# SwiGLU's gate and up as seven block products instead of eight, with the down projection in four chunks between the next chunk's pairs

## The chip, the cores and the metric

The kernel runs on one core of one Trainium2 chip. The metric is the device time of one execution in microseconds (us). Five engines matter here: TensorE (PE, with its weight loads listed apart as PEld), VectorE (DVE), ScalarE (ACT), GpSimd (POOL) and SyncE (SP), whose queue issues the loads. Each engine runs its own queue in order and waits on semaphores for the others.

## The reference

A decoder trunk of two layers on x of 512 tokens by 1024 features, all in float32:

```python
for i in range(2):
    x = x + 0.5 * swiglu(rmsnorm(x, ffn1_norm[i]), ffn1_w_gate[i], ffn1_w_up[i], ffn1_w_down[i])
    h = rmsnorm(x, mix_norm[i])
    o, o_mem = ...            # layer 0: gated linear attention, layer 1: latent attention; memory attention
    x = x + jnp.concatenate([o, o_mem], axis=-1) @ w_out[i]
    x = x + 0.5 * swiglu(rmsnorm(x, ffn2_norm[i]), ffn2_w_gate[i], ffn2_w_up[i], ffn2_w_down[i])

def swiglu(h, w_gate, w_up, w_down):
    return (jax.nn.silu(h @ w_gate) * (h @ w_up)) @ w_down
```

There are four SwiGLU blocks. In each, gate and up are 1024 x 2816 and down is 2816 x 1024.

## The kernel before

x lies transposed in SBUF: eight tiles of 128 features by 512 tokens, `x0` to `x7`. Every product keeps float32 accuracy by splitting both factors into a rounded high part and the exact rest: `mm3` issues three matmuls, high x high, high x low and low x high, all summed into one PSUM bank.

The weights come as a stream of units, 128 x 1024 each (eight blocks of 128 x 128). `load_unit` loads a unit into a `raw` tile through SP, `split_weights` makes `wh` (a cast on ACT) and `wl` (a subtraction on DVE). There are four slots for `wh` and four for `wl`, so splitting can run three units ahead of the one that PE is using.

A SwiGLU block (`ffn`) has two chunks of 11 blocks of 128 hidden features. For each block f, `project` sums the gate over the eight input tiles into one bank and the up into another; each takes one unit: 24 matmuls of 512 columns. `gate_up` scales by 1/rms, applies Silu, multiplies and splits the result. After 11 blocks the down projection runs over that chunk: for each of eight output tiles d, 11 blocks of three matmuls each, then `xadd` adds to x. The last chunk's `xadd` goes on into the next norm: `Norm.split` makes the scaled high and low parts of a tile (one ACT and one DVE instruction of 512), `Norm.square` adds up the squares, and `Norm.finish` gets 1/rms by Newton steps on DVE, whose result the gates wait for and PE does not.

The order of the instructions is planned: each of these pieces is a flow, a generator that yields instructions, and the flows are merged by the time at which an instruction could start by the planner's costs. The builder's own scheduler has the last word, and each engine then runs the result in order.

Of the kernel before, what the change touches and what calls it, by code (L numbers as in the profile page):

```python
# [17 lines left out]
P = 128  # L18
# [8 lines left out]
NCH = 2  # L27
FCH = NFT // NCH
# [9 lines left out]
NRAW, NSPL, NTMP = 3, 4, 64  # L38
NHEAD = 4
NLATE = 5  # L40

# [38 lines left out]
class Opening:  # L80
    """The first product into a bank that several flows sum into; the others come after it."""
# [23 lines left out]

class Engine:
    """An engine whose methods give instructions to be emitted later."""
# [4 lines left out]
    def __getattr__(self, method):  # L112
        real = getattr(self.eng, method)

        def make(*args, **kw):
            aps = [a for a in args if _is_ap(a)]
            outs = [kw[k] for k in ("out", "accum_out") if _is_ap(kw.get(k))]
            if "out" not in kw:
                outs.append(aps.pop(0))
            ins = aps + [v for k, v in kw.items() if k not in ("out", "accum_out") and _is_ap(v)]  # L120
            cost, lat = self.price(method, kw, outs, ins)
            return Op(self.name, lambda: real(*args, **kw), cost, [a.name for a in ins], [a.name for a in outs], lat)  # L122

        return make

    def price(self, method, kw, outs, ins):
        n = max([_n_free(outs[0])] + ([_n_free(ins[0])] if method == "tensor_reduce" else []))
        if self.name == "PE":
            passes = 1 if ins[0].dtype == F32R else 4
            n = _n_free(kw["rhs"]) if "rhs" in kw else P  # L130
            return passes * n / 2.4 + 3, 200
        if self.name == "ACT":
            return 110 + 0.833 * n, 200
# [9 lines left out]
        if single and not any(_in_psum(a) for a in ins[:1] + outs[:1]):  # L143
            return 60 + 0.65 * n, 130
        return 60 + 1.06 * n, 130


class Flows:
    def __init__(self, tiles):
        self.tiles = tiles  # kind -> (function of the dtype, slots)  # L150
        self.free_at = {k: deque([0.0] * n) for k, (_, n) in tiles.items()}
        self.kind, self.clock, self.wr, self.rd = {}, {}, {}, {}
        self.flows, self.count = [], 0
# [4 lines left out]

    def done(self, *tiles):
        for t in tiles:  # L160
            k = self.kind.pop(t.name)
            self.free_at[k].append(max(self.wr.get(t.name, 0.0), self.rd.get(t.name, 0.0)))
# [11 lines left out]
    def advance(self, f, value=None):  # L174
        """Runs a flow to its next instruction, wait or need."""
# [7 lines left out]
    def settle(self):  # L183
        """Gives the tiles and flags that can be given now."""
        moved = True
        while moved:
            moved = False
            for f in sorted(self.flows, key=lambda f: f[:2]):
                while True:
# [6 lines left out]
                    elif isinstance(w, Take) and len(self.free_at[w.kind]) > w.spare:  # L196
                        q = self.free_at[w.kind]
                        at = min(q)
                        q.remove(at)
                        t = self.tiles[w.kind][0](w.dt)  # L200
                        self.kind[t.name] = w.kind
                        self.rd[t.name] = at
# [7 lines left out]
    def run(self):  # L210
        while True:
# [4 lines left out]
            for f in self.flows:  # L216
                if isinstance(f[3], Op):
                    k = (self.start(f[3]), f[0], f[1])
# [17 lines left out]
def _emit(tc, ctx, xT, memT, wflat, sizes, cst, out):  # L236
    nc = tc.nc
    const = ctx.enter_context(tc.tile_pool(name="const", bufs=1))
    wraw = ctx.enter_context(tc.tile_pool(name="wraw", bufs=NRAW))
    wsp = ctx.enter_context(tc.tile_pool(name="wsp", bufs=NSPL))  # L240
# [6 lines left out]
        "t": (lambda dt: tp.tile([P, 512], dt, tag="t", name="t"), NTMP),  # L247
# [39 lines left out]
    units = [[Flag(), None, Flag(), None] for _ in sizes]  # L287
# [3 lines left out]
    def load_unit():  # L291
        u, n = units[ahead[0]], sizes[ahead[0]]
# [5 lines left out]
        u[1], u[0].set = raw, True  # L298

    def split_weights():  # L300
        for u, n in zip(units, sizes):
            yield u[0]
            h = yield Take("wh", F32R, 0)
            l = yield Take("wl", F32R, 0)
            yield A.copy(out=h[:, :n], in_=u[1][:, :n])
            yield V.tensor_tensor(out=l[:, :n], in0=u[1][:, :n], in1=h[:, :n].bitcast(F32), op=ALU.subtract)
            done(u[1])
            u[3], u[2].set = (h, l), True

    at = [0]  # L310
# [3 lines left out]
    class Blocks:  # L314
        """The next n blocks of the stream, w columns each, per blocks in a unit."""
# [4 lines left out]
        def next(self):  # L320
            j = self.i % self.per
            if j == 0:
                self.end()
                u = units[at[0]]
                assert sizes[at[0]] == min(self.per, self.n - self.i) * self.w, at
                at[0] += 1
                yield u[2]
                self.cur = u[3]
# [26 lines left out]
    def newton_rsqrt(dst, src, scale, hv, y, t):  # L355
        """dst = (src * scale + EPS) ** -0.5, of a guess from the exponent and Newton steps."""
# [13 lines left out]
    def wide_rsqrt(acc, n):  # L370
        """(the sum of acc over its partitions / n + EPS) ** -0.5, on all partitions."""
# [8 lines left out]
    def bcast(ps, col):  # L380
        """col [P tokens, NJ] -> ps [P, S], the value of each token on all partitions."""
# [10 lines left out]
    def colsum(ps, acc, n):  # L392
        """Sums over partitions of acc [P, n*P], onto the partitions of ps' columns."""
# [4 lines left out]
    class Norm:  # L398
        """x times the gain in two parts, and 1/rms of each token."""

        def __init__(self, gname, layer):
            self.g = (gname, layer * KD)
            self.layer, self.by_token = layer, gname == "mx"
            self.h, self.l = [None] * KD, [None] * KD
            self.part = [Flag() for _ in range(KD)]
            self.summed = [Flag() for _ in range(KD)]
# [3 lines left out]
        def add(self, k):  # L410
            yield from self.split(k)
            yield from self.square(k)

        def split(self, k):
            yield xin[k]
            lo = self.g[1] + k
            g = C(self.g[0], lo, lo + 1)
            h = yield tt(F32R)
# [3 lines left out]
            self.h[k], self.l[k], self.part[k].set = h, l, True  # L422

# [31 lines left out]
        def free(self):  # L455
            done(*self.h, *self.l)

    def project(ps, nrm):
        """ps [P features, S] = a column block of weights on the normed x (without 1/rms)."""
        blk = Blocks(KD, P, KD if at[0] else KD // NHEAD)  # L460
# [8 lines left out]
    def xadd(d, ps, scale, nxt, last):  # L469
        """x += scale * ps; what follows from it."""  # L470
# [13 lines left out]
    def ffn(nrm, nxt, last):  # L484
        def gate_up(f, pg, pu):
            yield nrm.ready
            g = yield tt()
            yield V.tensor_tensor(out=g, in0=pg, in1=nrm.bc, op=ALU.mult)
            done(pg)
            yield A.activation(out=g, in_=g, func=AF.Silu)  # L490
            u = yield tt()
            yield V.tensor_tensor(out=u, in0=pu, in1=nrm.bc, op=ALU.mult)
            done(pu)
            yield V.tensor_tensor(out=u, in0=u, in1=g, op=ALU.mult)
            done(g)
            h = yield tt(F32R)
            l = yield tt(F32R)
            yield from split(u, h, l)
            done(u)
            hid[f][1:] = [h, l]  # L500
            hid[f][0].set = True

        for c in range(NCH):
            hid = [[Flag(), None, None] for _ in range(FCH)]
            for f in range(FCH):
                pg = yield bank(1)
                yield from project(pg, nrm)
                pu = yield bank(1)
                yield from project(pu, nrm)
                spawn(gate_up(f, pg, pu))  # L510
            end = c == NCH - 1
            if end:
                nrm.free()
            blk = Blocks(KD * FCH, P, KD)
            for d in range(KD):
                ps = yield bank(1)
                for f in range(FCH):
                    wh, wl = yield from blk.next()
                    yield hid[f][0]
                    yield from mm3(ps, wh, wl, hid[f][1], hid[f][2], f == 0, f == FCH - 1)  # L520
                spawn(xadd(d, ps, 0.5, nxt if end else None, last and end))
            blk.end()
            for _, h, l in hid:
                done(h, l)
# [17 lines left out]
    def token_project(nrm, width, per, spare=2):  # L542
        """Projection with tokens on the partitions; as many tiles of tokens in a bank as fit."""
# [26 lines left out]
    def head_scale(ps, out, rs, rs2, m):  # L570
        """ps is raw [P tokens, 4 x 128], m tiles of tokens; out is ps with each 128 at an rms of 1."""
# [19 lines left out]
    def mem_prep(l, mp):  # L591
        """The memory times its gain in two parts, and 1/rms of its tokens."""
# [33 lines left out]
    class Mem:  # L626
# [93 lines left out]
        def half(self, h, b, po, ends, opening):  # L720
            """One head and two tiles of queries."""
# [91 lines left out]
    def gla(l, nrm, nxt):  # L813
# [15 lines left out]
        def decays(ps):  # L829
            """The gates' logarithms, summed within each chunk."""  # L830
# [32 lines left out]
        def head(h, pk, pq, pv):  # L863
# [40 lines left out]
            # scores of two chunks at a time, keys on the partitions  # L904
# [532 lines left out]
```

## Time and profile before

| what | value |
|---|---|
| time, median of 3 runs | 2079.43 us (2078.87 to 2079.77) |
| profiled execution, first to last instruction (span) | 2077.5 us |
| instructions | 24715 |
| PE / PEld busy | 2060.4 us (99%) / 1700.3 us (82%) |
| DVE busy | 1106.5 us (53%) |
| ACT busy | 723.1 us (35%) |
| POOL busy | 45.1 us (2%) |
| DMA | 192.76 MB, mean 93 GB/s |
| granted TensorE clock | 1.000 |

The profiled execution's own time is not listed beside the runs; its span is 1.9 us under their median, and the rest is what lies around the first and last instruction. Busy is the share of the span in which an engine works. Matmuls overlap, so the mean time of one (390 ns) is longer than the distance from one to the next, and a busy PE says only that there was always one in flight.

### The profile page before, as it was taken

The page shows a single profiled execution, that of the slowest core. Times are in us where ns is not written, and L with a number is a line of the kernel's source. Part 1 is how long each engine was busy: PE and PEld are TensorE (multiplying, and loading weights), DVE is VectorE, ACT ScalarE, POOL GpSimd, SP SyncE. Part 2 cuts the span into 40 slices and gives each one's busy share as a digit, 9 for nine tenths or more (in the row PEclk, how much of TensorE's full clock was granted, in tenths as well). Part 3 has the DMA queues.
Part 4 walks back from the last instruction along what each step waited for, and adds up shares of the span by engine and source line. Part 5 has one row for each costly group of instructions (what it writes and reads, how often), then busy time and mean ns, then how long its engine had stood idle before and what let it go on. Part 6 is the DMA issues. An engine that isn't in the chain of part 4 may idle for free.

```text
span 2077.5 us, 24715 instructions
## 1 busy us (share of the span) xinstructions
PE 2060.4 (99%) x9806; PEld 1700.3 (82%) x9806; DVE 1106.5 (53%) x1952; ACT 723.1 (35%) x1167; POOL 45.1 (2%) x121
## 2 busy tenths in 40 slices
PE   8999999999999999999999999999999999999999
PEld 6888888878988888888888888889876878888887
DVE  7443444548875744344464434445887657433442
ACT  5222233444442432223332223334576433222321
POOL 0000000000000000000000000000031100000000
PEclk9999999999999999999999999999999999999999
DMA  5323232313212223232333232323211213323231
GB/s 187 102 92 102 91 101 95 117 63 102 82 60 73 93 100 100 93 102 92 102 103 101 93 102 92 101 91 118 84 44 41 72 61 102 101 92 102 91 107 66
DMA packets 55988, 192.76 MB, mean 93 GB/s; under 512 B 6208, under 2 KB 8384, under 8 KB 55872
## 3 DMA queue, kind: packets, MB, share of 16 engines
q1 hardware_dynamic: 55584, 189.92, 27.9%
q8 instruction: 77, 1.26, 0.2%
q10 hardware_dynamic: 288, 1.26, 0.2%
q14 instruction: 39, 0.32, 0.0%
HBM read 189.05 MB, written 2.10 MB: 92 GB/s over the span
## 4 chain that ended last, share of the span: by engine, by line
PE 96%; DVE 2%; ACT 0%; issue 0%; DMA 0%; SPq 0%; POOL 0%; DVEq 0%; ACTq 0%
PE ps L122 96%; DVE s L122 1%; DVE wl L122 1%; DVE t L122 1%; ACT t L122 0%; DMA x<-xT 0%; SPq L122 0%; POOL t L122 0%; ACT wh L122 0%; DVE x L122 0%; DVE ps L122 0%; DVEq L122 0%; ACTq L122 0%
## 5 line engine op out<-in xcount | busy, mean ns | idle before, releaser
L122 PE MATMUL ps<-t,wh 128*128 128x512 f32 x4864 | 1507.4, 391 | 6.0 <-ACT wh L122 5.5
L122 PEld LDWEIGHTS ps<-t,wh 128*128 128x128 f32 x4864 | 912.5, 188 | 203.4 <-issue 6.7
L122 PE MATMUL ps<-t,wl 128*128 128x512 f32 x2432 | 949.1, 390 | 0.5 <-DVE wl L122 0.5
L122 ACT CAST wh<-raw 128x1024 fp32r<-128x1024 f32 (+3 forms) x361 | 370.0, 1027 | 1029.7 <-PE ps L122 650.3
L122 DVE TENSOR_TENSOR wl<-raw,wh 128x1024 fp32r<-128x1024 f32 (+3 forms) x361 | 430.0, 1192 | 243.0 <-ACT wh L122 242.5
L122 PEld LDWEIGHTS ps<-t,wl 128*128 128x128 f32 x2432 | 457.0, 188 | 97.3 <-issue 2.7
L122 DVE TENSOR_TENSOR t<-ps,t 128x512 f32<-128x512 f32 (+3 forms) x241 | 156.7, 656 | 471.9 <-PE ps L122 453.7
L122 PE MATMUL ps<-wh,t 128*128 128x256 f32 (+3 forms) x928 | 215.5, 320 | 0.0
L122 DVE TENSOR_TENSOR t<-t 128x512 f32<-128x512 f32 (+1 forms) x290 | 197.5, 688 | 11.9 <-ACT t L122 1.4
L122 PEld LDWEIGHTS ps<-wh,t 128*128 128x128 f32 x928 | 155.8, 190 | 10.2 <-issue 2.1
L122 PE MATMUL ps<-wl,t 128*128 128x256 f32 (+3 forms) x464 | 148.8, 321 | 0.0
L122 PE MATMUL ps<-t 128*128 128x128 f32 (+6 forms) x760 | 141.4, 329 | 0.9 <-ACT t L122 0.6
L122 DVE SCALAR_TENSOR_TENSOR x<-ps,x 128x512 f32<-128x512 f32 x96 | 66.0, 689 | 135.9 <-PE ps L122 135.9
L122 PEld LDWEIGHTS ps<-t 128*128 128x128 f32 (+1 forms) x760 | 98.0, 190 | 32.7 <-issue 16.9
L122 PEld LDWEIGHTS ps<-wl,t 128*128 128x128 f32 x464 | 88.3, 190 | 5.2 <-issue 1.1
L122 ACT ACTIVATE t<-t 128x512 f32<-128x512 f32 x124 | 76.2, 625 | 24.9 <-DVE t L122 24.8
L122 ACT CAST t<-t 128x512 fp32r<-128x512 f32 x96 | 59.9, 625 | 62.4 <-DVE t L122 62.4
L122 PE MATMUL ps<-cs,t 128*128 128x128 f32 x312 | 52.0, 276 | 5.7 <-DVE t L122 3.2
L122 PEld LDWEIGHTS ps<-cs,t 128*128 128x128 f32 x312 | 36.7, 141 | 21.6 <-issue 7.5
L122 ACT ACTIVATE t<-x,cs 128x512 fp32r<-128x512 f32 x48 | 34.3, 721 | 53.3 <-DVE x L122 49.4
L122 ACT COPY t<-ps 128x256 f32<-128x256 f32 (+3 forms) x86 | 36.3, 436 | 30.0 <-PE ps L122 26.7
L122 ACT ACTIVATE t<-ps 128x512 f32<-128x512 f32 (+3 forms) x64 | 30.3, 485 | 42.6 <-PE ps L122 42.5
(69 smaller groups left out, 558.7 us busy)
## 6 DMA issues: line engine op xcount, KB each, us to landing
raw<-wflat SPq DMA_DIRECT2D x341, 512.0 KB, 3.4
raw<-wflat SPq DMA_DIRECT2D x12, 192.0 KB, 2.4
x<-xT SPq DMA_DIRECT2D x8, 256.0 KB, 5.0
t<-memT SPq DMA_DIRECT2D x8, 256.0 KB, 4.1
out<-x SPq DMA_DIRECT2D x8, 256.0 KB, 2.0
raw<-wflat SPq DMA_DIRECT2D x4, 448.0 KB, 3.2
cm<-cst ACTq DMA_DIRECT2D x1, 640.0 KB, 4.1
cm<-cst ACTq DMA_DIRECT2D x1, 585.5 KB, 4.4
```

Source lines behind the costliest of these rows:

```text
L122: return Op(self.name, lambda: real(*args, **kw), cost, [a.name for a in ins], [a.name for a in outs], lat)
```

## The change

**Gate and up.** Two hidden blocks f, f+1 are taken together (a pair), and the product is done for both by 2 x 2 blocks: the weights are cut into an upper and a lower half of the input features and into gate and up; the normed x into an upper and a lower half of the features (tiles 0 to 3 and 4 to 7) and into the first and the last 256 tokens. Seven products of sums of such blocks replace the eight. One product has four input tiles by two hidden blocks, three matmuls each: 24 matmuls of 256 columns.

**Weights.** The four units of a pair arrive as they are. On DVE four additions of 128 x 1024 make the sums, and each of the seven factors is then split by a cast on ACT and a subtraction on DVE.

**The other factor.** `Norm` now makes seven sums of x (`SUMS`), each split, in pieces of 128 x 256: `upper` for tiles 0 to 3 gives two of them, `lower` for tiles 4 to 7 the other five.

**After the products.** p1 goes on as a summand of u2, u3 and p4 in the same bank, so ACT copies it out (`copy`) before the next product may write there; gate and up are put together in `gate` and `rest`.

**Down.** Four chunks of 4, 6, 4 and 8 blocks (`CHUNKS`). A chunk's down projection runs between the pairs of the next chunk, so many d after each pair (`SHARES`): 0, 0 | 2, 2, 4 | 4, 4 | 2, 2, 2, 2, and the last chunk's eight d at the end. `xadd` runs 32 times a block instead of 16.

**Besides.** Work tiles are 31 of 128 x 1024, given in halves, instead of 64 of 128 x 512. `raw` has four tiles instead of three. The first gate unit is loaded whole instead of in quarters, and the x tiles and units 0 to 3 are loaded in the order 0, x0 to x3, 1, x4, x5, 2, x6, x7, 3. In `w_out` the memory heads' rows move from the first part (6 + 4 blocks, then 2) to the second (6, then 4 + 2). The planner's costs, its bookkeeping of tiles by quarters, and the rank of `split_weights` differ.

```diff
-NRAW, NSPL, NTMP = 3, 4, 64
+NRAW, NSUM, NSPL, NTMP = 4, 2, 4, 31
+CHUNKS = (4, 6, 4, 8)
+SHARES = ((0, 0), (2, 2, 4), (4, 4), (2, 2, 2, 2))
 def split_weights():
...
+            u21, u22, u12 = (next(todo)[0] for _ in range(3))
...
+            yield from high(p, a11)
...
+            yield from add(s1, a21, a22)
+            yield from low(p, a11)
+            p = yield from parts()
+            yield from high(p, s1)
+            s2 = yield Take("sum", F32, 0)
+            yield from add(s2, s1, a11)
+            yield from low(p, s1)
...
+            yield from add(a21, a21, a11)
...
+            yield from add(s2, s2, a12)
...
+        def put(self, c, k, src):
...
+            yield A.copy(out=s[1], in_=src)
+            yield V.tensor_tensor(out=s[2], in0=src, in1=s[1].bitcast(F32), op=ALU.subtract)
...
+        def upper(self, j, k, g):
+            y = yield tt()
+            yield A.activation(out=y, in_=x[k], func=AF.Identity, scale=g)
...
+            yield from self.put("b11", j, y[:, :HS])
+            d = yield tt()
+            yield V.tensor_tensor(out=d[:, :HS], in0=y[:, :HS], in1=y[:, HS:], op=ALU.subtract)
+            yield from self.put("t1", j, d[:, :HS])
...
+        def gate(ps, name, other, half):
+            yield made_[name]
+            yield read[other]
+            g = got[other]
+            yield V.tensor_tensor(out=g, in0=ps, in1=g, op=ALU.add)
+            done(ps)
+            yield nrm.ready
+            yield V.tensor_tensor(out=both(g), in0=both(g), in1=scale(half), op=ALU.mult)
+            yield A.activation(out=g, in_=g, func=AF.Silu)
+            yield V.scalar_tensor_tensor(out=both(g), in0=both(g), scalar=-1.0, in1=scale(half), ...)
...
+        todo = [("p1", a, "b11", None), ("p5", b, "t1", None), ("u2", a, "t2", "p1"), ("p2", c, "b21", None),
+                ("u3", a, "t3", "u2"), ("p3", b, "b22", "p5"), ("p4", a, "t4", "u3")]
...
+        if start:
+            steps[2:4] = [(2, 0, KH - 1), (3, 0, KH - 1), (2, KH - 1, KH), (3, KH - 1, KH)]
...
+                if after is not None:
+                    yield read[after]
...
+                for i in range(2):
+                    w = slice((i * KH + k) * P, (i * KH + k + 1) * P)
+                    yield from mm3(ps[:, i * HS : (i + 1) * HS], wh[:, w], wl[:, w], x_part[1], x_part[2], ...)
...
+            for f in range(0, n, 2):
+                yield from seven(nrm, hid, f, c == 0 and f == 0)
+                yield from steps(before, SHARES[c][f // 2])
...
-        yield from project_out(o[: 2 * GH - 2] + mem.o, None)
-        yield from project_out(o[2 * GH - 2 :], nxt)
+        yield from project_out(o[: 2 * GH - 2], None)
+        yield from project_out(mem.o + o[2 * GH - 2 :], nxt)
...
-            if k % 2 == 0 and k // 2 < NHEAD:
+            if k in (3, 5, 7):
                 yield from load_unit()
```

The order in which the engines now run shows it at three places. The first is PE's queue at the program's start (`ps` a bank, `t` parts of x, `wh` and `wl` parts of weights). Before:

```order
L122 MATMUL ps_93<-t_95,wh_99 128x512 [waits Activation_49]
L122 MATMUL ps_93<-t_96,wh_99 128x512 [waits DVE_49]
L122 MATMUL ps_93<-t_95,wl_100 128x512
L122 MATMUL ps_93<-t_102,wh_99 128x512 [waits Activation_49]
L122 MATMUL ps_93<-t_103,wh_99 128x512 [waits DVE_49]
```

And in the changed kernel, its first product:

```order
L136 MATMUL ps_97<-t_105,wh_101 128x256 [waits Activation_49]
L136 MATMUL ps_97<-t_105,wh_101 128x256 [waits DVE_49]
L136 MATMUL ps_97<-t_105,wl_102 128x256
L136 MATMUL ps_97<-t_105,wh_101 128x256 x2
L136 MATMUL ps_97<-t_105,wl_102 128x256
```

Groups of three matmuls of 512 columns have become groups of three of 256, twice as many for the same x tile (two hidden blocks).

The second is DVE's queue at the program's start (`sum` the sums of weights, `raw` the loaded units). Before:

```order
L122 TENSOR_TENSOR wl_100<-raw_97,wh_99 128x256 [waits DMAHW2_49,Activation_49]
L122 SCALAR_TENSOR_TENSOR t_96<-x0_77,cs_73,t_95 128x512 [waits DMAHW1_49]
L122 SCALAR_TENSOR_TENSOR t_103<-x1_78,cs_73,t_102 128x512 [waits DMAHW3_49,Activation_49]
L122 TENSOR_TENSOR wl_128<-raw_107,wh_127 128x256 [waits DMAHW5_49,Activation_49]
L122 SCALAR_TENSOR_TENSOR t_106<-x2_79,cs_73,t_105 128x512 [waits DMAHW4_49]
```

And now, from the eleventh row on:

```order
L136 TENSOR_TENSOR sum_139<-raw_123,raw_128 128x1024 [waits DMAHW6_49,DMAHW1_49]
L136 TENSOR_TENSOR t_167<-t_104 128x256
L136 TENSOR_TENSOR sum_147<-sum_139,raw_96 128x1024 [waits DVE_49]
L136 TENSOR_TENSOR wl_144<-sum_139,wh_143 128x1024 [waits Activation_49]
L136 TENSOR_TENSOR t_106<-t_157,t_106 128x256 [waits Activation_49]
L136 TENSOR_TENSOR t_106<-t_167,t_106 128x256 [waits Activation_49]
```

The second product's factor (`wl_144`, of `sum_139`) now stands behind a sum that waits for the second and the third unit to land, `raw_123` and `raw_128`; PE's second product, on `ps_98`, is the first to use it.

The third is DVE's queue at the start of the second SwiGLU block, in the Newton steps of its norm (`t_5464` before and `t_6279` now among their tiles). Before:

```order
L122 TENSOR_SCALAR t_5464<-ps_5453 128x512 [waits PE_49]
L122 TENSOR_SCALAR t_5331<-t_5464 128x512 [waits DVE_49]
L122 TENSOR_SCALAR t_5464<-t_5464 128x512 [waits DVE_49] x2
L122 SCALAR_TENSOR_TENSOR t_5465<-t_5464 128x512 [waits DVE_49]
L122 TENSOR_TENSOR t_5465<-t_5465,t_5331 128x512 [waits DVE_49]
L122 TENSOR_TENSOR wl_5501<-raw_5442,wh_5500 128x1024 [waits DMAHW0_49,PE_49,Activation_49]
```

And now:

```order
L136 TENSOR_SCALAR t_6279<-ps_6542 128x512 [waits PE_49]
L136 TENSOR_TENSOR wl_6494<-sum_6319,wh_6493 128x1024
L136 TENSOR_TENSOR t_6252<-ps_6412,t_6252 128x512 [waits PE_49]
L136 TENSOR_SCALAR t_6163<-t_6279 128x512 [waits DVE_49]
L136 TENSOR_TENSOR wl_6562<-raw_6202,wh_6561 128x1024 [waits Activation_49]
L136 TENSOR_SCALAR t_6279<-t_6279 128x512 [waits DVE_49]
L136 TENSOR_TENSOR sum_6595<-raw_6489,raw_6521 128x1024 [waits DMAHW6_49,DMAHW5_49]
```

Where one unit's `wl` stood among the Newton steps, nearly every second row is now a factor of 128 x 1024 or a piece of a gate.

More of the change, by code (lines that the diff above doesn't have):

```diff
@@ L103, in _in_psum, with _places @@
     return a.space == bass.MemoryType.PSUM
+def _places(aps):
+    got = []
+    for a in aps:
+        row = int(a.ap[0][0]) if a.space != bass.MemoryType.DRAM else 0
+        lo = a.offset % row if row else 0
+        hi = lo + sum(abs(int(st)) * (int(n) - 1) for st, n in a.ap[1:])
+        got.extend((a.name, b) for b in range(lo // BLOCK, hi // BLOCK + 1))
+    return got
 class Engine:
@@ L121, in make @@
             cost, lat = self.price(method, kw, outs, ins)
[L122 removed]
+            return Op(self.name, lambda: real(*args, **kw), cost, _places(ins), _places(outs), lat)
         return make
@@ L195, in settle @@
                         self.advance(f)
[L196 to L202, printed above, removed]
+                    elif isinstance(w, Take) and (t := self.give(w)) is not None:
                         self.advance(f, t)
@@ L284, in small @@
         return sm.tile([P, 16], F32, tag="s", name="s")[:, :n]
-    units = [[Flag(), None, Flag(), None] for _ in sizes]
+    units = [[None, Flag()] for _ in sizes]
+    outs = [[Flag(), None, n] for n, four in sizes for _ in range(7 if four == 1 else 1 if four == 0 else 0)]
     ahead = [0, 0]
     def load_unit():
-        u, n = units[ahead[0]], sizes[ahead[0]]
+        u, n = units[ahead[0]], sizes[ahead[0]][0]
         raw = yield Take("raw", F32, 0)
@@ L297, in load_unit, with parts @@
         ahead[1] += n * P
-        u[1], u[0].set = raw, True
+        u[0], u[1].set = raw, True
     def split_weights():
-        for u, n in zip(units, sizes):
-            yield u[0]
+        def parts():
             h = yield Take("wh", F32R, 0)
             l = yield Take("wl", F32R, 0)
[L305 to L308, printed above, removed]
@@ L410, in add, with make_room @@
         def add(self, k):
+            spawn(self.square(k), 1)
             yield from self.split(k)
-            yield from self.square(k)
+        def make_room(self):
+            for k2 in range(KH // 2):
+                for c in self.SUMS[:2]:
+                    self.tiles[c, k2] = yield Take("d", F32R, 0)
+            self.room[0].set = True
+            for k2 in range(KH // 2):
+                for c in self.SUMS[2:]:
+                    self.tiles[c, k2] = yield Take("d", F32R, 0)
+            self.room[1].set = True
         def split(self, k):
@@ L417, in split @@
             g = C(self.g[0], lo, lo + 1)
+            if self.seven:
+                if self.room is None:
+                    self.room = [Flag(), Flag()]
+                    spawn(self.make_room(), 0)
+                yield from (self.upper if k < KH else self.lower)(k % KH, k, g)
+                self.part[k].set = True
+                return
             h = yield tt(F32R)
@@ L455, in free @@
         def free(self):
-            done(*self.h, *self.l)
+            if self.seven:
+                done(*self.tiles.values())
+            else:
+                done(*self.h, *self.l)
     def project(ps, nrm):
-        blk = Blocks(KD, P, KD if at[0] else KD // NHEAD)
+        blk = Blocks(KD, P, KD)
         for k in range(KD):
@@ new lines, in ffn, with down, steps @@
+    def ffn(nrm, nxt, last):
+        def down(hid, end):
+            n = len(hid)
+            blk = Blocks(KD * n, P, KD)
+            for d in range(KD):
+                ps = yield bank(1)
+                for f in range(n):
+                    wh, wl = yield from blk.next()
+                    yield hid[f][0]
+                    yield from mm3(ps, wh, wl, hid[f][1], hid[f][2], f == 0, f == n - 1)
+                spawn(xadd(d, ps, 0.5, nxt if end else None, last and end))
+                yield None
+            blk.end()
+            for _, h, l in hid[::2]:
+                done(h, l)
+        def steps(gen, n):
+            got = None
+            while n:
+                try:
+                    w = gen.send(got)
+                except StopIteration:
+                    return
+                got = None
+                if w is None:
+                    n -= 1
+                else:
+                    got = yield w
+        before = (None for _ in ())
+        for c, n in enumerate(CHUNKS):
+            hid = [[Flag(), None, None] for _ in range(n)]
+            for f in range(0, n, 2):
+                yield from seven(nrm, hid, f, c == 0 and f == 0)
+                yield from steps(before, SHARES[c][f // 2])
+            yield from steps(before, KD)
+            end = c == len(CHUNKS) - 1
@@ L512, in ffn @@
             if end:
                 nrm.free()
[L514 to L524, printed above, removed]
+            before = down(hid, end)
@@ L525, in ffn @@
+        yield from steps(before, KD + 1)
         done(nrm.bc)
@@ L1266, in start @@
         spawn(trunk(nrm), 2)
+        yield from load_unit()
         for k in range(KD):
@@ L1309, in _pack_weights, with put @@
 def _pack_weights(i):
-    us = []
+    us, four = [], []
+    def put(arrays, first=0):
+        us.extend(arrays)
+        four.extend(first if i == 0 or not first else -1 for i in range(len(arrays)))
     def cols(w):
```

300 lines of the change are left out of this document (237 added, 63 removed).

## The prediction

> **What bounds the kernel now.** I read the totals first, then the chain that ended last, then PE's waits, then stretches of steady work.
>
> ```profile
> PE 2060.4 (99%) x9806; PEld 1700.3 (82%) x9806; DVE 1106.5 (53%) x1952; ACT 723.1 (35%) x1167; POOL 45.1 (2%) x121
> PE 96%; DVE 2%; ACT 0%; issue 0%; DMA 0%; SPq 0%; POOL 0%; DVEq 0%; ACTq 0%
> PE ps L122 <- ACT wh L122: 5.5, 1, 5.5
> PE ps L122 <- DVE t L122: 3.7, 6, 1.3
> 15.99 479.27 PE ps L122 x2220
> 0.00:16.00 16.00, 9.43 (x27) 5.29 (x27) 9.33 (x18) 10.95 (x19) 0.20 (x4) 1.00 0.82 264
> ```
>
> The chain is PE's own work for 96%, its waits are a few microseconds (total, times, longest), and from 16 us on the chain is one unbroken piece of 479 us of matmuls. Only the start is different: 27 matmuls in 16 us. So matmul time is the price of everything, as long as DVE and ACT, at 53% and 35%, deliver on time. What a matmul costs is read as distance, since they overlap: the count in a full stretch.
>
> ```profile
> core 0: us, PE busy (x) PEld busy (x) DVE busy (x) ACT busy (x) POOL busy (x), PEclk, DMA share, GB/s
> 20.00:240.00 220.00, 220.00 (x970) 181.83 (x969) 104.46 (x127) 61.51 (x74) 0.00 (x0) 1.00 0.32 106
> 515.20:538.20 23.00, 23.00 (x193) 23.00 (x192) 21.14 (x58) 7.80 (x11) 0.00 (x0) 1.00 0.37 113
> L122 PE MATMUL ps<-t,wh 128*128 128x512 f32 x646 | 199.4, 390 | 0.0
> L122 PE MATMUL ps<-t,wl 128*128 128x512 f32 x322 | 125.3, 389 | 0.0
> L122 PE MATMUL ps<-wh,t 128*128 128x256 f32 x128 | 23.2, 283 | 0.0
> L122 PE MATMUL ps<-wl,t 128*128 128x256 f32 x64 | 18.1, 283 | 0.0
> ```
>
> In the first stretch 968 of 970 matmuls have 512 columns: 220/970 = 0.2268 us each. In the second (a token projection of the mixer) 192 of 193 have 256: 23.0/192 = 0.120 us. Both run at clock 1.00 with one weight load for each matmul.
>
> **The matmuls.** A pair of hidden blocks cost 2 x 2 x 24 = 96 matmuls of 512, 21.77 us; it now costs 7 x 24 = 168 of 256, 20.16 us. One eighth of the columns goes, but a matmul of 256 costs 53% of one of 512, so 1.61 us is saved and not 2.72. Four blocks of 11 pairs: 44 x 1.61 = **-71 us**. Down, mixers and clock: no change in matmuls.
>
> The weight load under the shorter matmul is where this could fail. The Trainium skill (TensorE: Matmul & The Clock Gate, in Part 3 under "What overlaps and what doesn't") says a weight load overlaps matmuls in flight only in another row group, which speaks against many short matmuls of full height. The row of 515 us disagrees: 192 loads of full height passed beside 192 matmuls at 0.120 us. By the rule the load would be added to each of the 7392 new matmuls and to the 4224 that they replace, and the change would end slower (the last rival but one below).
>
> **DVE and ACT, per pair.** What one instruction takes from the next is less than its own length:
>
> ```profile
> 485.30 3.69 DVE L122 TENSOR_TENSOR t<-t 128x512 f32<-128x512 f32 x6
> 488.91 3.49 DVE L122 TENSOR_TENSOR wl<-raw,wh 128x1024 fp32r<-128x1024 f32 x3
> L122 DVE TENSOR_TENSOR wl<-raw,wh 128x1024 fp32r<-128x1024 f32 x341 | 417.3, 1225 | 235.4 <-ACT wh L122 234.9
> L122 DVE TENSOR_TENSOR t<-t 128x512 f32<-128x512 f32 x193 | 131.6, 689 | 10.3 <-ACT wh L122 0.5
> L122 DVE TENSOR_TENSOR t<-t,s 128x256 f32<-128x256 f32 x32 | 13.8, 434 | 0.1
> L122 DVE TENSOR_SCALAR t<-t 128x512 f32<-128x512 f32 x4 | 1.7, 423 | 0.0
> 16.79 2.71 ACT L122 ACTIVATE t<-x 128x512 f32<-128x512 f32 x5
> 19.41 1.99 ACT L122 CAST wh<-raw 128x1024 fp32r<-128x1024 f32 x2
> L122 ACT COPY t<-ps 128x512 f32<-128x512 f32 x14 | 8.3, 590 | 11.4 <-PE ps L122 11.3
> 479.50:493.90 14.40, 14.40 (x77) 12.32 (x76) 14.23 (x21) 8.31 (x13) 0.00 (x0) 1.00 0.36 120
> 1440.00:1520.00 80.00, 77.77 (x479) 70.01 (x478) 69.14 (x287) 48.08 (x120) 9.54 (x22) 1.00 0.27 85
> ```
>
> Back to back, a DVE instruction of 512 takes (3.69-0.69)/5 = 0.60 us and one of 1024 (3.49-1.225)/2 = 1.13; the same slope gives 0.33 for 256 (an estimate). Standing alone they take 0.689, 1.225 and 0.434. On ACT, 512 takes (2.71-0.62)/4 = 0.52 and 1024 takes 1.99-1.05 = 0.94.
>
> A pair now has seven `wl` and four sums of 1024 and eleven instructions of 512 on DVE: 11 x 1.13 + 11 x 0.60 = 19.1 us (21.1 at full length) against 20.2 us of PE; before, 4 x 1.13 + 8 x 0.60 = 9.3 against 21.8. ACT has seven casts and eight instructions of about 0.5: 10.7 us, half of PE, at no cost. So DVE is level with PE wherever pairs follow each other without down products. A d of the down projection gives air: with four blocks 12 x 0.2268 = 2.72 us of PE for half a unit (0.57) and an `xadd` (0.60). The plan puts no d behind the first two pairs of a block and two behind the third; from the fourth pair on DVE gains: a pair with two d is 25.6 us of PE and 21.5 of DVE. So the risk sits in the first three and a half pairs of each block, with the norm's sums and Newton steps in the same queue.
>
> There I count DVE's rows in the changed order, up to the `wl` of the 26th unit (the fourth product of the fourth pair), where they lie furthest behind. PE's work before that unit is 24 products of 2.88, one unit of down of 5.44 and the norm's ones matmul (0.4): 75.0 us.
>
> *Second and fourth block*, counted from the end of the last product of `w_out`: 36 rows of 1024, 44 of 512, 14 of 256, four tensor-scalars: 40.7+26.4+4.6+1.7 = 73.4 us back to back, 82.3 at full length; 0.8 for the last `xadd` ahead makes 74.2 to 83.1. Late by -0.8 to 8. *Third block*: 33, 44, 12 and 4 rows: 70 to 78, late by -5 to 3. Which end? Dense stretches of this trace ran at 14.23/14.40 = 99% (21 instructions, few hand-offs) and at 69/80 = 86% (many). Some 30 of the 98 rows wait for ACT, so I take a third of the way: **+3, +1, +3 us**, none below zero.
>
> **The start.** Before, 27 matmuls (6.1 us) were done in 16 us: 9.9 us lost. The changed queue loads three whole units and six x tiles ahead of the sum that the second product needs (`sum_139`):
>
> ```profile
> 0.00:12.00 12.00, 6.15 (x15) 3.64 (x16) 5.58 (x12) 7.59 (x14) 0.20 (x4) 1.00 0.81 257
> 12.00:14.00 2.00, 1.93 (x9) 1.16 (x8) 2.00 (x5) 2.00 (x5) 0.00 (x0) 1.00 0.94 293
> raw<-wflat SPq DMA_DIRECT2D x341, 512.0 KB, 3.4
> x<-xT SPq DMA_DIRECT2D x8, 256.0 KB, 5.0
> cs<-cst SPq DMA_DIRECT2D x1, 102.0 KB, 2.0
> ```
>
> That is 102 + 3 x 512 + 6 x 256 KB = 3.25 MB. The rows moved 3.08 MB in 12 us and then 293 GB/s: landed at 12.6 us. From that sum to the `wl` of the 26th unit DVE has 41 rows of 1024, 51 of 512, 36 of 256 and four tensor-scalars: 46.3+30.6+11.9+1.7 = 90.5 us, 102.7 at full length. So the 26th unit is ready at 103 to 115 us, where PE needed 75.0: 28 to 40 lost instead of 9.9, **+18 to +30**; a third of the way, +22.
>
> **Costed at nothing.** 64 more `xadd` (0.60 each) lie beside down products, where DVE has air. The copies of p1, u2 and p5 must be out before the product after the next: cover 2.88 us of another product, need a cast ahead in ACT's queue (0.94) and the copy (0.59). Without that cover each would cost up to 1.5 us. SP has about as many loads of the same bytes; a fourth `raw` tile covers the four units that a sum holds. In `w_out` the last heads had 80 blocks of 3 x 0.2268 = 54 us of cover and now have 52 blocks, 35 us; their chain of softmax or gates is some ten instructions of 0.3 to 0.7, so 0, up to 5.
>
> **Sum** for the profiled execution: 2077.5 - 71 + 22 + 7 = 2035.5, and with the 1.9 us by which the median stands above the span, **2038 us**. Bounds of the unknown terms: 18 and 0 give 2026, 30 and 19 give 2058.
>
> **Rivals.**
> *DVE at full length.* If each instruction holds DVE until its end, as waits on ACT and on its own last result would do, the upper ends hold everywhere: 2077.5 - 71 + 30 + 8 + 3 + 8 + 1.9 = 2058. For it: about a third of the rows wait for ACT, and DVE's queue is in order. Against: the rows of six and of three above. The Trainium skill (VectorE: DVE Perf Modes, "The DRAIN you can't avoid") states that the next operation doesn't start until the pipe is empty; the trace disagrees for independent operations (0.60 of 0.689), and no row shows a queue as dense as the new one. By the rule the time would be this rival's.
>
> *ACT's copies stand in PE's way* (slower). Three times a pair, 132 times in all four blocks, PE may start a product only after ACT has copied the bank. If a second cast or an instruction that itself waits for DVE stands ahead of the copy, the cover of 2.88 us is used up, and PE waits. The saving that is left, 42 us, is gone at 42/132 = 0.32 us for each copy. At 0.5 us: 2038 + 66 = 2104. Against it: the 1.5 us needed leave 1.3 of the 2.88.
>
> *The weight load comes out* (slower too). The saving ends where a matmul of 256 costs 21.77/168 = 0.1296 us, only 8% above 0.120.
>
> ```profile
> L122 PEld LDWEIGHTS ps<-wh,t 128*128 128x128 f32 x928 | 155.8, 190 | 10.2 <-issue 2.1
> ```
>
> A load lasts 0.190 us from fetch to end; at that price 7392 x 0.07 = 517 us more. Against it stand 192 in a row at 0.120.
>
> *The front is hidden better*: units land sooner or nothing is late behind the first block: 2010 to 2026.
>
> **How the numbers follow.** Likeliest, 0.60: 2038, own range 2026 to 2050. DVE at full length, 0.22: 2058. Front hidden, 0.06: 2018. Copies in the way, 0.08, of which 0.05 end slower. Weight load, 0.02, half of it slower. No gain for another reason, 0.02. A difference of 0.2% is 4 us, about what can be told from none. Faster 0.92, same 0.02, slower 0.06. The range of 8 in 10 reaches from the hidden front into DVE at full length: 2020 to 2062.
>
> **What would show it.** Right: matmuls of 256 at 0.120 us where a block is past its fourth pair; DVE busy over 90% in the first 75 us of each block and some 75 to 80% over the span; PE's waits there put down to DVE (`wl` and `t`); the first 100 us short of 28 to 34 us of matmul work. Wrong: PE waiting for ACT in every pair, from the first chunk to the last; a distance over 0.125 us where nothing waits; or no wait at all behind the start.

## The result, and the profile after

The changed kernel takes 2034.09 us (median of 4 runs, 2033.31 to 2034.76) against 2079.43 (median of 4 too, 2078.87 to 2079.77): a ratio of 0.9782, interval 0.9768 to 0.9796. Forecast were 2038 us, range 2020 to 2062. The profiled execution spans 2032.6 us, 44.9 less than before. (One execution among the experiments, 4436.84 us in the run on `w_out`, ran PE at less than half its rate from end to end; it stands outside the comparisons, and that kernel's rows below are of another execution.)

Totals and shares of the chain:

```profile
PE 2001.6 (98%) x12974; PEld 1804.4 (89%) x12974; DVE 1595.5 (78%) x2597; ACT 983.2 (48%) x1584; POOL 49.1 (2%) x121
PE 87%; DVE 9%; issue 1%; ACT 1%; DMA 0%; SPq 0%; POOL 0%; ACTq 0%; DVEq 0%; POOLq 0%
```

PE is still the chain, but DVE, at 2% of it before, now has 9%. The longest pieces of the chain show where (start, length):

```profile
36.50 43.83 PE ps L136 x358
88.65 8.62 PE ps L136 x41
103.25 274.60 PE ps L136 x1821
772.01 640.90 PE ps L136 x4346
```

Before, PE ran unbroken from 16 us on; now from 103 us on, and the third and fourth piece are as unbroken as that one was. In stretches (columns as in the prediction: length, then busy time and count of PE, PEld, DVE, ACT, POOL, then clock, DMA share, GB/s):

```profile
16.00:40.00 24.00, 18.33 (x104) 16.51 (x105) 22.77 (x46) 19.02 (x41) 0.00 (x0) 0.79 0.23 72
40.00:84.00 44.00, 44.00 (x364) 43.52 (x364) 43.76 (x56) 22.92 (x30) 0.00 (x0) 1.00 0.36 118
84.00:103.30 19.30, 16.21 (x95) 14.00 (x93) 18.96 (x27) 8.95 (x13) 0.00 (x0) 0.91 0.12 37
60.00:80.00 20.00, 20.00 (x169) 20.00 (x168) 20.00 (x27) 10.93 (x15) 0.00 (x0) 1.00 0.32 108
12.82:106.06 93.24, 82.43 (x584) 77.30 (x583) 91.42 (x133) 54.80 (x88) 0.00 (x0) 0.93 0.28 93
700.00:775.00 75.00, 74.08 (x589) 72.24 (x589) 74.58 (x98) 43.01 (x61) 0.00 (x0) 1.00 0.30 99
1045.00:1120.00 75.00, 75.00 (x601) 73.65 (x600) 73.25 (x93) 41.41 (x55) 0.00 (x0) 1.00 0.35 114
1690.00:1765.00 75.00, 74.08 (x589) 72.24 (x588) 74.69 (x98) 43.00 (x60) 0.00 (x0) 1.00 0.30 99
```

Where nothing waits (60 to 80 us) 169 matmuls of 256 fit into 20 us; less the two or three that hang over the edges that is the 0.120 us of the old stretch. The first block loses in two places: before 40 us, and again from 84 to 103. At the fronts of blocks 2, 3 and 4 DVE is busy 98% to almost 100%, and PE misses under 1 us of busy time. What PE waits for in the first 110 us (total, times, longest):

```profile
PE ps L136 <- ACT t L136: 11.4, 5, 7.8
PE ps L136 <- DVE t L136: 2.9, 3, 1.2
PE ps L136 <- ACT wh L136: 2.7, 2, 1.5
PE ps L136 <- DVE wl L136: 1.5, 2, 0.9
```

The 7.8 is the very first matmul (5.5 before). From the same records I add up, by stage, what PE lost: the distance from each matmul to the next, less 0.2268 or 0.120 us for its size, and the wait for the first one. The mixers have matmuls of other sizes too; how these are priced moves a mixer's sum by several microseconds, but the differences between two kernels by 0.4 at most. The sums (us):

| kernel | block 1 | mixer 1 | block 2 | block 3 | mixer 2 | block 4 | all | span |
|---|---|---|---|---|---|---|---|---|
| before | 10.5 | 10.7 | 0.4 | 0.2 | 18.6 | 0.4 | 40.8 | 2077.5 |
| after | 31.1 | 13.7 | 1.9 | 0.7 | 17.9 | 1.9 | 67.2 | 2032.6 |

PE lost 26.4 us more and the span fell by 44.9, so the matmuls themselves gave 71.3. That is a remainder, which holds as far as 0.120 us does: block 3 lost only 0.7 us in all at that price. Lost time isn't idle time alone. In block 1 the waits listed above make 18.5 of the 31.1 us; some 8 us of the rest are matmuls that followed each other at about half their rate (the last section has the rows).

### The profile page after: what moved, and what is told of

Its sections match the earlier page's. It is cut to its first block, busy times and chain, and to the rows that moved or that the text cites. A ratio compares the mean times of both kernels' runs of the same rounds, so it can differ in the third digit from the quotient of the medians.

```text
span 2032.6 us, 32247 instructions
## 1 busy us (share of the span) xinstructions
PE 2001.6 (98%) x12974; PEld 1804.4 (89%) x12974; DVE 1595.5 (78%) x2597; ACT 983.2 (48%) x1584; POOL 49.1 (2%) x121
## 4 chain that ended last, share of the span: by engine, by line
PE 87%; DVE 9%; issue 1%; ACT 1%; DMA 0%; SPq 0%; POOL 0%; ACTq 0%; DVEq 0%; POOLq 0%
PE ps L136 87%; DVE t L136 4%; DVE wl L136 3%; DVE s L136 2%; DVE sum L136 1%; ACT t L136 1%; ACT wh L136 0%; DMA raw<-wflat 0%; DVE raw L136 0%; DVE x L136 0%; SPq L136 0%; POOL t L136 0%; DVE ps L136 0%; DVE rs L136 0%; ACTq L136 0%
## 5 line engine op out<-in xcount | busy, mean ns | idle before, releaser
L136 PE MATMUL ps<-t,wh 128*128 128x256 f32 (+1 forms) x6976 | 1537.8, 316 | 18.9 <-ACT t L136 12.5
L136 PEld LDWEIGHTS ps<-t,wh 128*128 128x128 f32 x6976 | 1158.0, 192 | 109.3 <-ACT t L136 13.8
L136 PE MATMUL ps<-t,wl 128*128 128x256 f32 (+1 forms) x3488 | 1100.8, 316 | 1.6 <-DVE wl L136 1.5
L136 PEld LDWEIGHTS ps<-t,wl 128*128 128x128 f32 x3488 | 668.2, 192 | 45.1 <-issue 3.5
L136 ACT CAST wh<-raw 128x1024 fp32r<-128x1024 f32 (+2 forms) x358 | 368.7, 1031 | 501.3 <-PE ps L136 379.1
L136 DVE TENSOR_TENSOR wl<-raw,wh 128x1024 fp32r<-128x1024 f32 (+2 forms) x358 | 428.5, 1199 | 112.1 <-ACT wh L136 111.4
L136 DVE TENSOR_TENSOR t<-t 128x512 f32<-128x512 f32 (+3 forms) x522 | 307.8, 611 | 13.6 <-ACT t L136 10.0
L136 ACT CAST wh<-sum 128x1024 fp32r<-128x1024 f32 x132 | 138.4, 1048 | 159.7 <-PE ps L136 108.9
L136 DVE TENSOR_TENSOR wl<-sum,wh 128x1024 fp32r<-128x1024 f32 x132 | 160.9, 1219 | 55.4 <-ACT wh L136 55.4
L136 ACT COPY t<-ps 128x512 f32<-128x512 f32 (+3 forms) x262 | 138.9, 534 | 58.9 <-PE ps L136 54.2
L136 PEld LDWEIGHTS ps<-t 128*128 128x128 f32 (+1 forms) x760 | 99.1, 191 | 27.4 <-issue 12.6
L136 DVE SCALAR_TENSOR_TENSOR t<-t 128x512 f32<-128x512 f32 (+1 forms) x172 | 108.6, 634 | 12.8 <-ACT t L136 12.2
```

The source lines that it names most:

```text
L136: return Op(self.name, lambda: real(*args, **kw), cost, _places(ins), _places(outs), lat)
```

## The experiments

Theory A says: the matmuls gave 71 us, and what was lost of that is DVE's queue, which at the front of each block, above all the first, holds more than PE's work covers. The rivals: ACT's casts and copies, which two of the four lines of waits above name (B in the expectations); the start and the half clock in it, whatever DVE does (C); and that some of the gain is the interleaved down projection.

**The down projection alone.** The kernel before with `CHUNKS`, `SHARES` and the loop over them, gate and up unchanged:

```diff
-NCH = 2
+CHUNKS = (4, 6, 4, 8)
+SHARES = ((0, 0), (2, 2, 4), (4, 4), (2, 2, 2, 2))
```

> The kernel before with the down projection alone changed (chunks of 4, 6, 4 and 8 blocks, run between the next chunk's blocks); gate and up stay eight ordinary products. Theory A (all of the gain is the seven products' 71 us of matmuls, the interleaving is only cover for DVE): 2077 to 2083. Rival (part of the gain is the interleaving): under 2075.

Measured: 2079.61 us, ratio 1.000 (0.9991 to 1.001). The interleaving by itself gives nothing. The kernel before lost only 0.4 us in block 2 and 0.4 in block 4, so the order of `w_out` had next to nothing to save there either: the gain is the seven products' matmuls.

**No sums of weights.** Each factor that was a sum becomes one of its summands:

```diff
-            s1 = yield Take("sum", F32, 0)
-            yield from add(s1, a21, a22)
-            yield from high(p, s1)
+            yield from high(p, a22)
```

> Leaves out the four additions of weights per pair: the seven factors are plain units instead of sums, so the output is another. DVE has 4 x 1.13 us less per pair, ACT and PE have the same work. Theory A (in the first block PE follows DVE's queue): about 16 of the 41 rows of 1024 up to the 26th unit go, so of the 31 us that PE loses in the first block 16 to 18 go, and the 3 us of the other blocks: 2034 becomes 2014 to 2018. Rival B (PE waits for ACT's copies and casts, as the waits are named): nothing to speak of, 2030 to 2035. Rival C (the start and the half clock in it cost the time, whatever DVE does): at most 5 us less, 2029.

Measured: 2020.75 us, ratio 0.9717 (0.9702 to 0.9731), 13.3 faster. Of it 9.9 are in block 1 (31.1 to 21.2 lost) and 2.7 in blocks 2 and 4; the second loss of block 1 is gone:

```profile
84.00:103.30 19.30, 19.30 (x149) 18.68 (x149) 11.80 (x15) 9.28 (x12) 0.00 (x0) 1.00 0.33 114
```

So the sums on DVE are the cause of the second loss, and B and C, which expected 2029 or more, are both off. But A had expected 3 to 7 us more: 21 us stay lost in block 1, in the first 50 us, where units and x tiles land and the first parts are made. Which of these holds PE up there without the sums is not shown.

**One sum made twice**, 1.13 us more of DVE in each of 44 pairs:

```diff
             yield from add(s1, a21, a22)
+            yield from add(s1, a21, a22)
```

> The first sum of each pair is made twice: 1.13 us more of DVE per pair, 50 us in all, nothing else. Theory A: it counts only in the first three and a half pairs of each block, where DVE is level with PE: +4 to +5 in the first block, about +4 in the second and fourth, +2 in the third: 2047 to 2050. If DVE bound the whole of gate and up: 2034 + 44 x 1.13 = 2084. If DVE had air (rivals B, C): 2034 to 2036.

Measured: 2047.42 us, ratio 0.9844 (0.9829 to 0.9859), 13.3 slower, where 44 x 1.13 = 50 us of DVE were added. Block 1 lost 6.8 more, blocks 2 and 4 4.1 each, block 3 0.4: DVE bounds the fronts and has room behind them, as A says.

**Two of the four sums on POOL:**

```diff
-            yield from add(a21, a21, a11)
+            yield from add(a21, a21, a11, G)
...
-            yield from add(s2, s2, a12)
+            yield from add(s2, s2, a12, G)
```

> Two of the four sums of weights of a pair (the ones needed for the fifth and the sixth product) are made by POOL instead of DVE. DVE has 2.3 us less per pair. Theory A: half of what leaving out all four brings in the first block, 8 to 9 us, and the 3 us of the others: 2022 to 2026, unless POOL's rate (2.3 to 4 us for one sum, an estimate from its rows of 64 and 128) makes these sums late. Rivals B and C: 2029 to 2035. A further way: POOL and DVE get in each other's way in SBUF, then DVE's instructions get longer and it is slower than 2034.

Measured: 2080.12 us, ratio 1.0002 (0.9992 to 1.0012): the whole gain was gone. The groups of the changed kernel, then of this one (count | busy, mean ns | idle before):

```profile
L136 DVE TENSOR_TENSOR wl<-raw,wh 128x1024 fp32r<-128x1024 f32 x342 | 417.7, 1223 | 111.4 <-ACT wh L136 111.1
L136 DVE TENSOR_TENSOR t<-t 128x512 f32<-128x512 f32 x281 | 189.8, 685 | 3.9 <-PE ps L136 1.3 <-ACT t L136 0.7
```

```profile
L136 DVE TENSOR_TENSOR wl<-raw,wh 128x1024 fp32r<-128x1024 f32 x342 | 475.8, 1396 | 108.8 <-ACT wh L136 108.1
L136 DVE TENSOR_TENSOR t<-t 128x512 f32<-128x512 f32 x281 | 233.7, 840 | 4.0 <-PE ps L136 1.3 <-ACT t L136 0.6
L136 POOL TENSOR_TENSOR sum<-sum,raw 128x1024 f32<-128x1024 f32 x44 | 150.4, 3417 | 368.9 <-DVE wl L136 352.9 <-ACT wh L136 8.3 <-issue 7.7
L136 POOL TENSOR_TENSOR raw<-raw 128x1024 f32<-128x1024 f32 x44 | 131.5, 2989 | 779.7 <-DVE sum L136 556.4 <-ACT t L136 191.0 <-DMA raw<-wflat 23.8
```

POOL needs 3.0 to 3.4 us for what DVE does in 1.22, and while it works DVE's own instructions are longer: in the trace the 69 DVE rows of 1024 that overlap one of POOL's sums last 2.13 us on average, the longest 3.44, and the other 493 last 1.22. DVE made 88 sums fewer and was busy 1635.1 us, more than before the edit. The Trainium skill says (SBUF — State Buffer, "Who interferes with whom") that a DVE instruction with two inputs in SBUF contends with a GpSimd instruction that reads SBUF, and that the port pair they share is an exclusive lock; the longer rows agree. How much of the 46 us is this and how much the later sums was not separated.

**ACT's copies made twice** (`copy`, four a pair):

```diff
             yield A.copy(out=got[name], in_=ps)
+            yield A.copy(out=got[name], in_=ps)
```

> ACT copies each bank that another product goes on in, or that gate and up take later, twice (some 0.5 us more of ACT, several times a pair; the values are the same). Theory A (DVE's queue at each block's front sets the loss, ACT has room): 2034 to 2039, a few microseconds at the front alone. Rival B (the copies stand in PE's way between products): each second copy is paid by PE, up to 132 x 0.5 = 66 us: 2055 to 2100.

Measured: 2032.71 us, ratio 0.9774 (0.9759 to 0.9788), no different from the changed kernel's.

```profile
PE 1999.7 (99%) x12974; PEld 1802.8 (89%) x12974; DVE 1596.6 (79%) x2597; ACT 1080.3 (53%) x1760; POOL 48.1 (2%) x121
```

ACT took on 97 us and PE none of it, so the copies are not what PE waits for. Its casts are no better a rival: ACT has as many instructions (1584) in the run without sums, where the second loss is gone. In that loss ACT's own rows in the changed kernel say why it was late (in brackets its idle time and what ended it):

```profile
85.77 0.62 ACT L136 CAST t<-t 128x512 fp32r<-128x512 f32 x1 [2.31 <-DVE t L136]
87.56 1.04 ACT L136 CAST wh<-sum 128x1024 fp32r<-128x1024 f32 x1 [1.17 <-DVE sum L136]
```

ACT stood idle before both casts until DVE had made what they read.

**Down products at the chunk's end.** All eight d behind the last pair of the next chunk:

```diff
-SHARES = ((0, 0), (2, 2, 4), (4, 4), (2, 2, 2, 2))
+SHARES = ((0, 0), (0, 0, 8), (0, 8), (0, 0, 0, 8))
```

> The down products of a chunk no longer run between the next chunk's pairs, but all eight behind the last pair but one, or the last, of that chunk; the work is the same. Theory A (DVE is level with PE in pairs without down products between them, and any air that it has is used up in a row of them): PE waits some more in chunks 2 to 4, 0.5 to 1 us for each pair without air: 2036 to 2050. Rival (the interleaving gives nothing, DVE at 19.1 us a pair against 20.2 of PE keeps up by itself): 2031 to 2036.

Measured: 2027.4 us, ratio 0.9746 (0.9731 to 0.976): 6.7 faster, where A had expected 2 to 16 slower. The same stretches as above, of this kernel:

```profile
84.00:103.30 19.30, 19.30 (x163) 19.30 (x162) 19.30 (x25) 12.03 (x16) 0.00 (x0) 1.00 0.29 92
40.00:150.00 110.00, 110.00 (x828) 105.76 (x828) 109.47 (x137) 55.84 (x72) 0.00 (x0) 1.00 0.33 108
```

The second loss is gone: block 1 lost 24.4 and not 31.1, block 3 half a microsecond more, blocks 2 and 4 0.7 less each. In the changed kernel it begins here, in PE's rows:

```profile
86.44 0.98 PE L136 MATMUL ps<-t,wh 128*128 128x512 f32 x4 [0.37 <-ACT t L136]
88.65 0.39 PE L136 MATMUL ps<-t,wh 128*128 128x256 f32 x1 [1.24 <-ACT wh L136]
103.25 0.39 PE L136 MATMUL ps<-t,wl 128*128 128x256 f32 x1 [0.93 <-DVE wl L136]
```

The matmuls of 512 at 86.44 are the two d behind the third pair. They need the hidden parts of the first two pairs, so DVE has to make gates before the fourth pair's factors. With no d there, the same DVE delivers factors at PE's pace (163 matmuls in 19.3 us, DVE 100% busy) and makes the gates later. The d that I had counted as air for DVE are air only once their hidden parts are done; in the first block they come too early.

**`w_out` in its old order**, the rest changed:

```diff
-        yield from project_out(o[: 2 * GH - 2], None)
-        yield from project_out(mem.o + o[2 * GH - 2 :], nxt)
+        yield from project_out(o[: 2 * GH - 2] + mem.o, None)
+        yield from project_out(o[2 * GH - 2 :], nxt)
```

> The memory heads' rows of w_out go back to the first part (6 + 4 blocks, then 2), the rest stays changed. The second part then has 2 blocks for each output tile and not 6, so the norm's sums at the front of blocks 2 and 4 have 8 x 4 x 3 x 0.2268 = 22 us less of PE's work beside them. Theory A (DVE's queue at the front of a block sets what is lost there): blocks 2 and 4 lose 6 to 20 us more together, the mixers 0 to 3 less: 2037 to 2054. Rival (those sums are hidden in any case): 2030 to 2035.

Measured: 2053.98 us (median of three), ratio 0.9876 (0.9859 to 0.9892), 20 us slower than the changed kernel. For the stages:

> The same kernel as in the run on w_out, for a profile by stage (the one taken there ran with PE at less than half its rate from end to end). Theory A (the norm's sums of blocks 2 and 4 have lost their cover): some 20 us more of lost PE time stand in the first 75 us of blocks 2 and 4 (from about 600 and from about 1620 us on), the mixers are within 3 us. Rival: they stand in the mixers.

Measured: 2055.24 us.

```profile
700.00:775.00 75.00, 69.03 (x508) 65.55 (x506) 73.32 (x108) 41.62 (x64) 0.00 (x0) 0.93 0.26 85
1690.00:1765.00 75.00, 69.03 (x511) 65.68 (x510) 73.52 (x117) 48.37 (x80) 0.00 (x0) 0.93 0.23 77
```

Block 2 lost 12.8 and block 4 12.6, against 1.9 each; the mixers 13.7 and 17.8, as they were. So the longer second part of `w_out` is worth 20 us of time (21.6 of lost work), all at the fronts of these two blocks, where the norm's sums are made.

**The second and third unit ahead of x4** in the order of loads:

```diff
-            if k in (3, 5, 7):
+            if k == 3:
+                yield from load_unit()
+                yield from load_unit()
+            if k == 7:
```

> The changed kernel with the second and third unit loaded together right behind x3, ahead of x4 to x7. If the landing of the third unit (the start of the first sum, 12.8 us) sets where DVE's queue begins: that sum starts about 1.5 to 3 us sooner, and the time is 2031 to 2033. If the other factor's sums of x4 to x7, now later, take its place: 2034 or more.

Measured: 2031.25 us, ratio 0.9768 (0.9754 to 0.9783), 2.8 faster. The first sum starts at 11.71 and not at 12.82 us, 1.1 sooner where 1.5 to 3 had been expected, released by its load:

```profile
11.71 1.22 DVE L136 TENSOR_TENSOR sum<-raw 128x1024 f32<-128x1024 f32 x1 [0.82 <-DMA raw<-wflat]
```

The landing is at most a small part of the start's loss: block 1 lost 29.4, which is 1.7 less. Even that is not clear of what block 1 varies by: it lost 29.1 with the copies made twice and 30.0 with the old `w_out`, edits that leave the loads alone.

**The first two pairs as ordinary products**, with the first unit in quarters again, and the seven sums of x made meanwhile:

```diff
-                yield from seven(nrm, hid, f, c == 0 and f == 0)
+                if first and c * 10 + f // 2 < NPLAIN:
+                    yield from plain(nrm, hid, f)
...
+                else:
+                    yield from seven(nrm, hid, f, c == 0 and f == 0)
```

> Undoes the seven products in the first two pairs of the first block alone, with the loads at the start as they were before the change; the seven sums of x are made meanwhile. Theory A: PE loses 10.5 us at the start as before the change instead of 31, and pays 2 x 1.6 us for the two plain pairs, while DVE has 2 x 12 us of air for the sums: 2034 - 20.5 + 3.2 = 2017, and up to 2022 if the sums come a little late. If the loss belongs to the first pairs of seven products wherever they stand: it moves to the third pair, 2030 to 2036.

Measured: 2018.03 us, ratio 0.9702 (0.9688 to 0.9717), 16.1 faster than the changed kernel.

```profile
12.00:40.00 28.00, 27.01 (x116) 21.18 (x115) 27.25 (x51) 21.86 (x42) 0.00 (x0) 1.00 0.50 175
40.00:84.00 44.00, 44.00 (x288) 40.43 (x287) 43.95 (x69) 25.59 (x42) 0.00 (x0) 1.00 0.27 89
```

Block 1 lost 11.2, nearly as little as before the change (10.5), though DVE is as busy as ever: two pairs with 9.3 us of DVE each beside 21.8 of PE gave it the time to catch up.

**One ordinary pair:**

```diff
-NPLAIN = 2
+NPLAIN = 1
```

> Only the first pair of the first block is made of eight ordinary products, not two. An ordinary pair has 9.3 us of DVE beside 21.8 of PE, one of seven 19.1 beside 20.2: air of 11.4 us for each ordinary pair. The first block lost 31 us without one and 11 with two. If DVE's arrears are what is lost: 31 - 11.4 = 20 with one, and 1.6 us of matmuls saved: 2018 + 9 - 1.6 = 2025. If one is enough to get past the start: 2016.

Measured: 2028.77 us, ratio 0.9756 (0.9742 to 0.9772), between the two expected times and 3.8 above the nearer; block 1 lost 21.4, where 20 had been expected. From no ordinary pair to two it lost 31.1, 21.4 and 11.2: 10 us for each pair, where the arithmetic of DVE's time said 11.4.

**Both gains together**, against the kernel with two ordinary pairs:

```diff
-SHARES = ((0, 0), (2, 2, 4), (4, 4), (2, 2, 2, 2))
+SHARES = ((0, 0), (0, 0, 8), (0, 8), (0, 0, 0, 8))
```

> Both edits that gained: the first two pairs of the first block as eight ordinary products, and each chunk's down products all behind the last pair of the next chunk. If both removed the same lateness of DVE in the first block: 2016 to 2018 (block 2 alone may gain another microsecond). If they are independent gains, they add up: 2018 - 7 = 2011.

Measured: 2016.34 us, ratio 0.9698 (0.9684 to 0.9713), block 1 11.0. The interval overlaps the one of ordinary pairs alone, so the two remove the same arrears and do not add up. It is the fastest here, 63 us under the kernel before; of its 46 lost microseconds 32 are in the mixers and 11 at the start.

## Why the prediction was right

- **The matmuls:** -71 forecast, -71.3 by subtraction, with the distance at 0.120. The rival in which the weight load comes out between shorter matmuls fell: 168 loads passed beside 169 matmuls in 20 us.
- **The start:** +22 forecast (18 to 30), +20.6 measured. DVE's rows, counted from the first sum (12.6 forecast, 12.82 measured) to the 26th unit, gave 90.5 us back to back and 102.7 at full length; DVE took 93.24, a fifth of the way, where I took a third. The end of the wait, with DVE's rows there:

```profile
101.97 1.22 DVE L136 TENSOR_TENSOR wl<-sum,wh 128x1024 fp32r<-128x1024 f32 x1
103.11 0.68 DVE L136 TENSOR_TENSOR t<-t 128x512 fp32r<-128x512 f32 x1
104.85 2.35 DVE L136 TENSOR_TENSOR wl<-raw,wh 128x1024 fp32r<-128x1024 f32 x2
```

  The 25th factor is ready at 103.19, and PE resumes at 103.25 on `wl`; the 26th, ready at 106.07, comes as PE needs it. So the place was right too, and 106.07 less the 75.0 us of PE's work is the 31.1 that block 1 lost. What was not right: the d behind the third pair stood in my sum as 5.44 us of cover, and the run with them at the end shows that they bring DVE's gates forward and cost 6.7. The count held because those rows were in it, whatever the reason that they stood there; in that part the number was luck.
- **Blocks 2, 3, 4:** +3, +1, +3 forecast, +1.5, +0.5, +1.5 measured. DVE is nearer to back to back (74.58 of 75 us busy) than a third of the way. The terms were also drawn too large: a third of the way from -0.8 to 8 is 2.1 and from -5 to 3 below zero, and I had taken a third of the upper ends. And the place was right only in part: in block 2, which starts at 695 us, 0.6 of the 1.9 lost stand at 772 us, where the 26th unit was forecast, and 1.2 at 705 to 709 us, about 10 us into the block.
- **Costed at nothing:** the copies and `xadd` were right. The mixers were set at 0 (up to 5) and came to +3.0 and -0.7. I had put a loss there down to `w_out`'s order; the run with the old order leaves it at 13.7, so it is another of the changes. The interleaving isn't it either: with that alone the first mixer loses what it lost before, within 0.1 us. Which one it is stays open. What I did not price is that the new order of `w_out` saves 20 us at blocks 2 and 4.
- **The sum:** -71.3 + 20.6 + 3.0 + 1.5 + 0.5 - 0.7 + 1.5 = -44.9; forecast -42.
- **The rivals.** DVE at full length (2058) fell with DVE's 93.24 us. The Trainium skill's sentence behind it (VectorE: DVE Perf Modes, "The DRAIN you can't avoid") taken alone gives a too long time here; the same section adds that an operation that is not held starts earlier. The rows agree with the addition, in the new, dense queue too: the one at 103.11 starts 1.14 us after the one at 101.97, which lasts 1.22. The copies fell with their doubling. The front hidden better was not this kernel, but its 2010 to 2026 is where the version with two ordinary pairs lands.
- **What would show it:** DVE's shares came as said (98% in the first front, 78% over the span), and so did the lost work. The name of the wait did not: I said DVE, and the profile says ACT for most of it. In the second loss the last releaser is a cast on ACT that had itself waited for DVE; the largest wait, the 7.8 us before the first matmul, I had not counted as DVE's.

## What to carry to other kernels

When a change trades matmuls for vector work, count the other engine's rows up to the point where they lie furthest behind, and lay them against PE's work up to there; shares over the whole span (78% here) hide it. Spend the saving where the other engine has air: at the start of a program, an ordinary product that needs fewer preparations is cheaper than the clever one (16 us here, at 1.6 us of matmuls a pair). Work put in between to give air must not itself depend on what the late engine still owes, and a wait that names one engine is traced back one step further before that engine is blamed.

## What the runs showed of the hardware

The granted clock fell to half in steps where PE stopped and went. Four stretches of the changed kernel, three of them of 3.4 us, around the two d behind the third pair:

```profile
82.00:85.80 3.80, 3.80 (x34) 3.80 (x33) 3.80 (x7) 1.27 (x3) 0.00 (x0) 1.00 0.52 153
85.80:89.20 3.40, 1.79 (x11) 1.29 (x10) 3.40 (x5) 1.63 (x2) 0.00 (x0) 1.00 0.40 137
89.20:92.60 3.40, 3.40 (x11) 2.77 (x10) 3.40 (x7) 1.59 (x3) 0.00 (x0) 0.50 0.00 0
92.60:96.00 3.40, 3.40 (x25) 3.13 (x24) 3.40 (x6) 0.90 (x2) 0.00 (x0) 1.00 0.00 0
```

After 3.4 us in which PE was busy for 53%, with no single wait over 1.24 us, the clock is 0.50 for the next 3.4 us, in which PE is always busy: its matmuls of 512 columns follow each other at about 0.42 us there, not 0.227. (That 25 pass behind them and not 11 is only in part the clock; most of the 25 have 256 columns.) It happens at the start too (0.51 from 17.5 to 24.4 us) and not at all in the version with two ordinary pairs between 12 and 84 us. The very first matmuls also pass at about half the rate, though the clock's column says 1.00 there: 18 of 256 columns in 4 us, 0.22 us each.

```profile
8.00:12.00 4.00, 4.00 (x18) 3.83 (x19) 2.20 (x7) 3.09 (x7) 0.00 (x0) 1.00 1.01 371
```

The half clock is no rival for the loss of block 1 in the changed kernel. From the first sum to the 26th factor, 12.82 to 106.06 us, DVE was busy 91.42 of 93.24 us, and PE then went on with DVE's factors. A full clock would have brought PE to the same waits sooner and could have saved at most the 1.8 us in which DVE stood still.
